# A transformer layer with 32 experts on one core: first gather from raw rows, logits by halves, a shorter root, and the overflow branch ahead of the scaling

## The chip, the core and the metric

The kernel runs on one core of a Trainium2 chip. It is timed on the device, in microseconds (us), as the median of several executions. Its engines are named as the profile names them: PE (TensorE matmul), PEld (TensorE's weight load, which overlaps PE), DVE (VectorE), ACT (ScalarE), POOL (GpSimd) and SP (SyncE, which here only issues DMAs; "SPq" is its queue, as "PEq" is PE's sequencer). A weight piece is 1 MB.

## The reference

One layer over 256 tokens of width 1024 (and 256 context tokens that only carry a state forward). All arrays are float32.

```python
sh1, sc1, gt1, sh2, sc2, gt2 = _split_mod(jax.nn.silu(c) @ w_mod + b_mod)
hx = _rms_norm(x, g_norm1) * (1.0 + sc1) + sh1
ux = hx @ w_in
...                     # a gated delta rule in two directions over ctx, then over x
mix_x = jnp.concatenate([_fourier(ux[..., :FOURIER_W]), _gated_out(ox, zx, g_out_norm)], axis=-1) @ w_out
x = x + gt1 * mix_x
h2x = _rms_norm(x, g_norm2) * (1.0 + sc2) + sh2
# mixture of experts: 32 experts, 4 for each token
logits = h @ w_router + b_router
top_v, top_i = lax.top_k(logits, 4)
gates = softmax(top_v)
# for each expert, on its tokens:
a = jnp.minimum(xb @ w_gate[e] + b_gate[e], 7.0)
u = jnp.clip(xb @ w_up[e] + b_up[e], -7.0, 7.0)
y = (a * sigmoid(1.702 * a) * (u + 1.0)) @ w_down[e] + b_down[e]
x = x + gt2 * sum(gate * y)
return _rms_norm(x, g_final)
```

Each of w_gate[e], w_up[e] and w_down[e] is 1024 x 1024, so the 32 experts have 384 MB of weights, and each is read once.

## The kernel before

The program has three parts.

**Prologue.** Modulation rows, norms, w_in, the delta rule, the Fourier products and w_out. It is cut into some forty small generators (`parts`), and a string `ORDER` and a table `EV` (which engine takes which copy out of PSUM) set the order in which they are recorded; a list scheduler of the framework then places their instructions by its own costs. The last parts are `X0` and `X1` (`routed`, L912): for each half `a` of 128 tokens it finishes x + gt1 * mix (L829, L830), multiplies by the norm's gain (L921: `xg`, the rows without the norm's factor), sums the squares on ScalarE (L922), turns `xg` by PE transposes (L927), copies the result (L199 or L201) and multiplies it by w_router (L933, 16 matmul records for 8 matmuls). `T` (`late_rows`, L939) spreads two rows of gt2 over the partitions with PE (L298), a ScalarE copy (L299) and GpSimd scalings (L946, L949).

**The hand-written bridge**, from L1217 on. From here the order on each engine is the written one. It takes the norm's factor `r` by `rsqrt` (L130: a first guess from the bits of the exponent and three Newton steps on VectorE, 11 operations in all). It then has PE multiply the rows by a diagonal matrix of `r` (`rows_`, L1228), while VectorE makes the logits (L1227), the top four and their mask (L1233 to L1239) and PE counts each token's rank within its expert (L1241 to L1245). `cast` (L1248) takes the scaled rows apart into three bfloat16 parts `h2s` whose sum is the row; the remainder for the next part is formed by PE (L1255, minus identity). `gather_first` (L1095) collects expert 0's tokens: a matmul with a one-hot matrix of the ranks, for 3 parts, 2 halves and 8 blocks of the width, 48 matmuls.

**The experts**, a loop of 32 (L1368), 64 token slots in the main path. Per expert: the gate's bias (L1123) and product (L1129, four weight pieces), its clip (L1135) and activation, the up product (L1129 again, four pieces), the gather for a later expert (L1091), the hidden rows turned (L1148), the down product (L1157, four pieces) and VectorE's scaling of its result by gt2/2 (L1422) into `yp`, which is later added into the token sums `yacc` by a matmul (L1207). An expert with more than 64 tokens takes a branch in two halves, for 32 further slots:

```python
if e >= EARLY:
    with tc.If(vs[e] > MAIN, preferred_fallthrough_block=False):
        hidden32(e, w)          # L1373, ahead of the gate's bias
...
if e >= EARLY:
    with tc.If(vs[e] > MAIN, preferred_fallthrough_block=False):
        down32(w)               # L1392, behind the up product
```

`hidden32` (L1162) builds a one-hot (L1073, L1075), gathers (L1091), does gate and up together (L1176, 64 matmuls), clips and activates (L1180 to L1184), then turns the gates (L1148) and the hidden rows and copies them. `down32` (L1193) has the down product (L1196).

**The weights** are loaded by SyncE alone, in order (`load_chunk`, L969), into 19 places that are used in turn. Most are old buffers of the prologue; one of them is the block "mm". SyncE waits until the last reader of a place is done, then issues the load and goes on to the next piece; all later pieces stand behind it.

Of the kernel before, what the change touches and what calls it, by code (L numbers as in the profile page):

```python
# [20 lines left out]
D = 1024  # L21
# [71 lines left out]
for _n, _w in (("c", 8), ("cc", 8), ("g1", 8), ("conv", 60), ("gout", 1), ("alog", 16), ("dtb", 16), ("br", 32)):  # L93
# [15 lines left out]
EV = {"fm0": "s", "mh01": "g", "ft1": "v", "md06": "v", "fm2": "s", "iu014": "v", "iu002": "s", "vn00": "s", "xT100": "v", "iu105": "s", "ip01": "v", "xh00": "s", "md04": "v", "xT110": "v", "md03": "v", "vn11": "v", "kT011": "v", "mh10": "v", "ir00": "s", "vv01": "s", "fa2": "s", "vv12": "v", "iu113": "s", "ix00": "s", "ft0": "s", "md05": "s", "fm3": "v", "xT010": "v", "md15": "v", "ir10": "v", "vv11": "v", "ir01": "s", "md02": "s", "iu104": "v", "iu004": "s", "md07": "v", "qg0": "s", "md17": "v", "xh10": "v", "mod0": "v", "kT101": "s", "iu103": "s", "xh11": "v", "mod2": "v", "ip00": "v", "xh01": "v", "xT011": "s", "cv100": "s", "xT001": "s", "mh00": "g", "cv201": "v", "iz11": "s", "cv113": "s", "cv103": "v", "iu112": "s", "iu111": "v", "cv010": "s", "fa1": "s", "kT111": "s", "qg1": "v", "ip10": "v", "vv10": "s", "iu011": "s", "qg2": "s", "iu114": "s", "fm1": "v", "cv211": "s", "cv213": "s", "cv013": "v", "md14": "s", "iu115": "v", "fa3": "v", "ip11": "v", "cv210": "v", "cv110": "v", "md00": "s", "cv212": "s", "ix10": "s", "xT000": "s", "md01": "s", "ix11": "v", "mh11": "g", "vv00": "v", "iu101": "v", "iu102": "v", "vn10": "s", "cv112": "v", "iz01": "v", "ix01": "v", "abT0": "v", "cv012": "v", "cv101": "s", "md11": "s", "mod1": "v", "qg3": "s", "iu005": "v", "xT101": "v", "md13": "s", "vv02": "s", "cv111": "v", "xT111": "s", "fa0": "v", "iu003": "s", "g21": "v", "md12": "s", "vv03": "v", "vn01": "s", "mh101": "s", "cv200": "s", "mh100": "v", "mh111": "g", "cv202": "s", "ir11": "g", "md10": "v", "g20": "s", "mh110": "v", "vv13": "s", "gT00": "v", "cv102": "v", "gT10": "v", "cv011": "v", "iz10": "s", "iu012": "s", "md16": "v", "mh011": "v", "iz00": "g", "cv203": "s", "mh001": "s", "mr24": "v", "mr25": "g", "mr23": "g", "mr27": "v", "mr10": "v", "kT110": "v", "mr26": "v", "gT11": "s", "mh010": "s", "kT010": "v", "kT100": "s", "mr11": "g", "mh000": "s", "mr22": "v", "iu015": "v", "mr14": "g", "iu001": "s", "mr21": "v", "gT01": "v", "iu013": "v"}  # L109
# [5 lines left out]
def body(ctx, tc, x, cx, sv, rows, cf, mk, w_mod, w_in, w_ab, w_out, w_router, w_exp, b_gate, b_up, b_down,  # L115
# [15 lines left out]
    def rsqrt(dst, v, scale, eps, mul=1.0):  # L131

        n = v.shape[-1]
        w = small.tile([128, n], F32, name="rsw")
        r = small.tile([128, n], F32, name="rsr")
        t = small.tile([128, n], F32, name="rst")
        nc.vector.tensor_scalar(w, v, scale, eps, op0=OP.mult, op1=OP.add)  # L137
        nc.vector.tensor_scalar(r.bitcast(I32), w.bitcast(I32), -0.5, float(0x5f3759df), op0=OP.mult, op1=OP.add)  # L138
        for i in range(3):
            nc.vector.tensor_tensor(t, r, r, OP.mult)  # L140
            nc.vector.scalar_tensor_tensor(t, t, -0.5, w, op0=OP.mult, op1=OP.mult)  # L141
            nc.vector.scalar_tensor_tensor(dst if i == 2 and mul == 1.0 else r, t, 1.5, r, op0=OP.add, op1=OP.mult)  # L142
        if mul != 1.0:
            nc.vector.tensor_scalar(dst, r, mul, None, op0=OP.mult)
# [752 lines left out]
    pl = None  # L897
# [14 lines left out]
    def routed(a):  # L912
        nonlocal pl
# [4 lines left out]
        for f in range(2):  # L918
# [20 lines left out]
    def late_rows():  # L939
# [3 lines left out]
        tmp = part("zfb", 0, D)  # L943
        for i in range(2):
            spread(tmp[:, 512 * i:512 * i + 512], mods[2], 64 + 32 * i)
            nc.gpsimd.tensor_scalar(g2h[64 * i:64 * i + 64], tmp[64 * i:64 * i + 64, 512 * i:512 * i + 512], 0.5, None,  # L946
                                    op0=OP.mult)
            for j in (2 * i, 2 * i + 1):
                nc.gpsimd.tensor_scalar(g2q[32 * j:32 * j + 32], tmp[32 * j:32 * j + 32, 256 * j:256 * j + 256], 0.5, None,  # L949
                                        op0=OP.mult)  # L950
# [93 lines left out]
    nib = keep.tile([128, 128], BF, name="nib")  # L1044
    nc.gpsimd.tensor_scalar(nib, ident, -1.0, None, op0=OP.mult)
# [49 lines left out]
    def gather_first(p, s, a):  # L1095

        for k in range(8):
            nc.tensor.matmul(p[:, k], h2s[:, s, a, 128 * k:128 * k + 128], ohs[0][:, a, 0], start=(a + s + k == 0),
                             stop=(a + s == 3), skip_group_check=True)
# [386 lines left out]
```

## Time and profile before

| | |
|---|---|
| median of 3 runs | 1300.39 us (1294.61 to 1303.88) |
| the profiled execution's own time | 1300.49 us |
| its span in the trace | 1298.4 us |
| PE busy | 1177.8 us, 91% |
| DVE, ACT, POOL busy | 415.8, 177.9, 91.8 us |
| mean granted clock of PE | 0.97 |
| moved by SyncE's DMA queue | 446.79 MB |

The span is the time from the first to the last record of the trace. The granted clock is the share of full speed that the chip allows TensorE. A busy share is an average over stages with different limits, so it doesn't say what ends the kernel; the rows below do. Times in the rows are counted from the span's start.

### The profile page before, as it was taken

To read this page: it belongs to the slowest core of one execution; us is meant where nothing else is said; L and a number is where in the kernel's file an instruction comes from. 1 tells how busy PE (TensorE), PEld (TensorE's weight loads), DVE (VectorE), ACT (ScalarE), POOL (GpSimd) and SP (SyncE) were. 2 spreads that over 40 slices of the span, in tenths; PEclk is the share of its full clock that TensorE was granted. 3 is DMA by queue.
4 is the path that set the end of the run, shared out by engine and by line. 5 is a ranking of instruction groups with operands and counts; after the bars stand their busy time and mean duration, and the time that the engine had idled before them with its cause. 6 is when DMAs were issued, how large, how long until landed. Compare 5 with 4: busy or idle time off the path is not lost. (4 is left out here: it accounts for less than half of the span.)

```text
span 1298.4 us, 17968 instructions
## 1 busy us (share of the span) xinstructions
PE 1177.8 (91%) x7381; PEld 534.3 (41%) x7381; DVE 415.8 (32%) x877; ACT 177.9 (14%) x338; POOL 91.8 (7%) x84
## 2 busy tenths in 40 slices
PE   6989988999989998989998998999789999998995
PEld 3767766665333333333332333333233333333322
DVE  2499879756311222111121211221122121221112
ACT  2165545111200000000000000000000000000001
POOL 1032544312000000000000000000000000000000
PEclk8999999999989999999999999999889999999998
DMA  9711353766799998899999999999999999999993
GB/s 383 273 33 67 120 174 111 288 249 238 313 355 418 420 419 328 354 420 418 418 421 418 420 419 419 419 420 419 419 420 421 419 420 419 419 420 419 418 416 116
DMA packets 65155, 450.60 MB, mean 347 GB/s; under 512 B 9220, under 2 KB 9608, under 8 KB 11000
## 3 DMA queue, kind: packets, MB, share of 16 engines
q1 hardware_dynamic: 64048, 446.79, 84.7%
q8 instruction: 106, 1.74, 0.5%
q10 hardware_dynamic: 904, 1.67, 0.3%
q14 instruction: 33, 0.27, 0.1%
q0 software_dynamic: 64, 0.13, 0.0%
HBM read 447.51 MB, written 1.05 MB: 345 GB/s over the span
## 5 line engine op out<-in xcount | busy, mean ns | idle before, releaser
L1129 PE MATMUL pg<-w,schT 128*64 128x512 f32 x1024 | 240.7, 616 | 17.7 <-issue 17.2
L1129 PE MATMUL pu<-w,schT 128*64 128x512 f32 x1024 | 229.4, 592 | 2.2 <-DMA w<-in_w_exp 2.1
L1157 PE MATMUL pd<-w,scA 128*64 128x512 f32 x1024 | 228.0, 598 | 1.1 <-ACTq L1373 0.7
L1129 PEld LDWEIGHTS pg<-w,schT 128*64 128x64 f32 x1024 | 74.9, 142 | 162.3 <-issue 153.9
L1129 PEld LDWEIGHTS pu<-w,schT 128*64 128x64 f32 x1024 | 73.1, 137 | 145.5 <-issue 131.5
L1157 PEld LDWEIGHTS pd<-w,scA 128*64 128x64 f32 x1024 | 70.9, 137 | 145.0 <-issue 136.7
L1422 DVE TENSOR_TENSOR xnat<-pd,qn 64x512 f32<-64x512 f32 x64 | 44.1, 688 | 269.6 <-PE pd L1157 269.1
L1135 DVE TENSOR_SCALAR schT<-pg 128x512 f32<-128x512 f32 x32 | 22.1, 692 | 247.1 <-PE pg L1129 247.1
L1136 ACT ACTIVATE scvnc<-schT 128x512 f32<-128x512 f32 x32 | 20.1, 630 | 547.6 <-DVE schT L1135 547.6
L1141 DVE TENSOR_SCALAR scvnc<-pu 128x512 f32<-128x512 f32 x32 | 22.1, 692 | 150.7 <-PE pu L1129 150.7
L1091 PEld LDWEIGHTS <-h2s 128*128 128x128 bf16 x864 | 45.2, 98 | 48.7 <-PEq L1392 40.3
L1207 PE MATMUL y<-xnat,scgm 128*128 128x512 f32 x136 | 61.3, 593 | 2.3 <-DVE xnat L1201 2.3
L1149 ACT ACTIVATE scA<-pg 128x512 f32<-128x512 f32 x32 | 19.1, 597 | 276.4 <-PE pg L1148 276.3
L507 PE MATMUL u<-hT,w 128*128 128x256 f32 x192 | 52.8, 402 | 0.0
L1091 PE MATMUL m<-scA,h2s 128*128 128x128 bf16 (+1 forms) x480 | 27.2, 212 | 12.5 <-PEq L1392 7.7
L507 PEld LDWEIGHTS u<-hT,w 128*128 128x128 f32 x192 | 33.2, 191 | 8.1 <-issue 4.3
L1207 PEld LDWEIGHTS y<-xnat,scgm 128*128 128x128 f32 x136 | 24.4, 190 | 27.7 <-issue 26.6
L317 ACT ACTIVATE w<-w,cst 128x256 f32<-128x256 f32 x80 | 33.9, 501 | 11.7 <-DMA w<-in_w_mod 11.7
L1082 DVE TENSOR_TENSOR schT<-m,sh2c 128x512 f32<-128x512 f32 (+2 forms) x33 | 22.2, 675 | 38.0 <-PE m L1091 37.3
L1123 PE MATMUL pg<-bgu,idb 96*64 96x512 bf16 x64 | 13.4, 417 | 21.3 <-PEq L1373 17.5
L1091 PE MATMUL m<-scgm,h2s 128*128 128x128 bf16 (+1 forms) x384 | 22.6, 215 | 8.9 <-PEq L1392 8.2
L318 POOL TENSOR_TENSOR w<-w 128x1024 f32<-128x1024 f32 x10 | 24.3, 2426 | 87.4 <-ACT w L317 87.4
(368 smaller groups left out, 1097.4 us busy)
## 6 DMA issues: line engine op xcount, KB each, us to landing
w<-in_w_exp SPq DMA_DIRECT2D x384, 1024.0 KB, 19.8
w<-in_w_mod SPq DMA_DIRECT2D x24, 1024.0 KB, 7.5
w<-in_w_in SPq DMA_DIRECT2D x6, 1024.0 KB, 6.4
w<-in_w_out SPq DMA_DIRECT2D x4, 1024.0 KB, 8.9
wk<-in_w_in SPq DMA_DIRECT2D x2, 1024.0 KB, 13.5
wv<-in_w_in SPq DMA_DIRECT2D x2, 1024.0 KB, 12.2
w<-in_cx SPq DMA_DIRECT2D x2, 512.0 KB, 5.1
xnat<-in_x SPq DMA_DIRECT2D x4, 256.0 KB, 12.8
```

Source lines behind the costliest of these rows:

```text
L317: nc.scalar.activation(w[:, k], w[:, k], AF.Copy, scale=sil[:, k, 0:1])
L318: nc.gpsimd.tensor_tensor(w[:, 0:4], w[:, 0:4], w[:, 4:8], OP.add)
L507: nc.tensor.matmul(p[:, c, :], w[c2][:, k, 128 * c:128 * c + 128], hT[:, k, 256 * n:256 * n + 256], start=(k == 0), stop=(k == 7))
L1082: nc.vector.tensor_tensor(dst[:, k0:k1], p, sh2c[:, k0:k1, None].to_broadcast([128, k1 - k0, p.shape[-1]]), OP.add)
L1091: nc.tensor.matmul(p[:, i], h2s[:, s, a, 128 * k:128 * k + 128], o[a], start=(s + a == 0), stop=(s + a == 3))
L1129: nc.tensor.matmul(p[64 * g:64 * g + 64], xg[:, k], w[k // 2][:, k % 2, 512 * g:512 * g + 512], start=False, stop=(k == 7), skip_group_che ...
L1135: nc.vector.tensor_scalar(a, p, 7.0, None, op0=OP.min)
L1136: nc.scalar.activation(hs_, a, AF.Tanh, scale=0.851)
L1141: nc.vector.tensor_scalar(hu_, p, 7.0, -7.0, op0=OP.min, op1=OP.max)
L1157: nc.tensor.matmul(p[64 * g:64 * g + 64], hT_[:, k, 64 * i:64 * i + 64], w[8 + 2 * i + k // 2][:, k % 2, 512 * g:512 * g + 512], start=(i ...
L1207: nc.tensor.matmul(yacc[a][g], ot[:, a, :], y[:, g, :], start=False, stop=False, skip_group_check=True)
L1422: nc.vector.tensor_tensor(yp[MAIN * j:MAIN * j + MAIN, g, :], p[hs], g2h[hs], OP.mult)
```

## The change

Six edits.

1. `routed` multiplies each turned half of the rows by its half of w_router at once, into the token sums' own PSUM (`yacc`), in place of all eight blocks at the end.
2. `late_rows` moves from the prologue's string into the bridge. PE spreads the two rows as before, and ScalarE scales them straight out of PSUM; GpSimd has no part in it.
3. `rsqrt` has nine operations in place of eleven (twelve, where a factor was applied).
4. The diagonal product, the copies behind it and the minus identity go. The first gather takes the raw rows `xg` in float32, with a one-hot `ohr` that holds the norm's factor where it held 1: 16 matmuls, four and four before the gate's product and eight within it. `ohr` lies in the block "mm".
5. The rows are taken apart into the three bfloat16 parts behind expert 0's gate product, by ScalarE and VectorE alone (`split`).
6. `hidden32(e + 1)` stands at the end of expert e, ahead of the scaling. Its gates and the turning of its hidden rows move into `down32`.

```diff
-    "H13 Fo E w Fo O0 O1 Fo w Lo Fo O0 X1 X0*2 w*2 X1 X0 T P w X1 X0 w X0 w*7 ")
+    "H13 Fo E w Fo O0 O1 Fo w Lo Fo O0 P X1 X0*2 w*2 X1 X0 w X1 X0 w*8 ")
...
-        for i in range(3):
-            nc.vector.tensor_tensor(t, r, r, OP.mult)
-            nc.vector.scalar_tensor_tensor(t, t, -0.5, w, op0=OP.mult, op1=OP.mult)
-            nc.vector.scalar_tensor_tensor(dst if i == 2 and mul == 1.0 else r, t, 1.5, r, op0=OP.add, op1=OP.mult)
-        if mul != 1.0:
-            nc.vector.tensor_scalar(dst, r, mul, None, op0=OP.mult)
+        c = 0.375 * mul
+        nc.vector.tensor_tensor(t, r, r, OP.mult)
+        nc.vector.scalar_tensor_tensor(t, t, -0.5 * c, w, op0=OP.mult, op1=OP.mult)
+        nc.vector.scalar_tensor_tensor(r, t, 1.5 * c, r, op0=OP.add, op1=OP.mult)
+        nc.vector.tensor_tensor(t, r, r, OP.mult)
+        nc.vector.scalar_tensor_tensor(t, t, 1.0 / (c * c), w, op0=OP.mult, op1=OP.mult)
+        nc.vector.scalar_tensor_tensor(t, t, -10.0 / 3.0, t, op0=OP.add, op1=OP.mult)
+        nc.vector.scalar_tensor_tensor(dst, t, 5.0, r, op0=OP.add, op1=OP.mult)
...
-            yield
-        if a == 0:
-            pl = bank("t", 2, 32)
-        for k in range(8):
-            nc.tensor.matmul(pl[:, a], xgT[:, k, :], wr[:, k, :], start=(k == 0), stop=(k == 7))
-        yield
+            for k in range(4 * f, 4 * f + 4):
+                nc.tensor.matmul(yacc[0][a][:, :32], xgT[:, k, :], wr[:, k, :], start=(k == 0), stop=(k == 7),
+                                 skip_group_check=True)
+            yield
...
+    def gather_first(p, ks):
+
+        for i, k in enumerate(ks):
+            for a in range(2):
+                nc.tensor.matmul(p[:, i], xgs[a][:, 128 * k:128 * k + 128], ohr[:, a], start=(a == 0), stop=(a == 1),
+                                 skip_group_check=True)
+
+    def split(a, f):
+
+        x, fs = xgs[a][:, 512 * f:512 * f + 512], slice(512 * f, 512 * f + 512)
+        nc.scalar.activation(x, x, AF.Copy, scale=r[:, a:a + 1])
+        yield
+        nc.vector.tensor_copy(h2s[:, 0, a, fs], x)
+        nc.vector.tensor_tensor(x, x, h2s[:, 0, a, fs], OP.subtract)
+        yield
+        nc.scalar.activation(h2s[:, 1, a, fs], x, AF.Copy)
+        yield
+        nc.vector.tensor_tensor(x, x, h2s[:, 1, a, fs], OP.subtract)
+        yield
+        nc.scalar.activation(h2s[:, 2, a, fs], x, AF.Copy)
+        yield
...
-        gates_turned(og, ovg)
-        p = mps.tile([128, 4, 64], F32, name="m")
+        return oh
+
+    def down32(e, w, oh):
+        gates_turned(gated(e, 1, oh, 4), ovg)
+        p = mps.tile([128, 4, 64], F32, name="pg")
...
+        next(parts["T"])
...
+        ohr = part("mm", 0, 2, MAIN)
+        for a in range(2):
+            nc.vector.tensor_scalar(ohr[:, a], io1[:, :MAIN], rk[:, a, 0:1], r[:, a:a + 1], op0=OP.is_equal, op1=OP.mult)
...
-            times(pg_, w[0:4], xg)
+                for p, ks in firsts:
+                    shifted(xg, p, ks)
+                times(pg_, w[0:4], xg, range(0, 2))
+                p = mps.tile([128, 4, MAIN], F32, name="pd")
+                gather_first(p, range(4, 8))
+                shifted(xg, p, range(4, 8))
+                times(pg_, w[0:4], xg, range(2, 8))
+                ohs[0] = onehot(oh_[0], 0, 2, 0, MAIN)
+                todo = [split(a, f) for a in range(2) for f in range(2)]
+                for i in range(len(todo) + 4):
+                    for j_, g in enumerate(todo):
+                        if 0 <= i - j_ < 5:
+                            next(g)
+            else:
+                times(pg_, w[0:4], xg)
...
             load_ahead(4)
+            if e + 1 < E:
+                with tc.If(vs[e + 1] > MAIN, preferred_fallthrough_block=False):
+                    ohov = hidden32(e + 1, weights_[e + 1])
             for g, hs in enumerate(halves):
                 nc.vector.tensor_tensor(yp[MAIN * j:MAIN * j + MAIN, g, :], p[hs], g2h[hs], OP.mult)
```

PE's instructions at the end of the prologue, in the order of the kernel before. `u` are the output product's tiles, `t` with `mm,cfk` the spread rows, `t` with `xg` the transposes, `t` with `gm` or `vec` the logits, `y` the diagonal product:

```order
L826 MATMUL u<-w,mixG 128x512
L298 MATMUL t<-mm,cfk 128x512 x2
L826 MATMUL u<-w,mixG 128x512 x4
L927 MATMUL t<-cfk,xg 128x128 x4
L933 MATMUL t<-mm,gm 128x32 x8
L927 MATMUL t<-cfk,xg 128x128 x4
L933 MATMUL t<-mm,vec 128x32 x8
```

The same place in the changed kernel, where the logits are L930 and the spread rows L944, both in the token sums' tiles `y`:

```order
L828 MATMUL u<-w,mixG 128x512
L930 MATMUL y_2937<-mm,gm 128x32 x4
L930 MATMUL y_2938<-mm,vec 128x32 x4
L828 MATMUL u<-w,mixG 128x512 x4
L927 MATMUL t<-cfk,xg 128x128 x4
L930 MATMUL y_2937<-mm,gm 128x32 x4
L927 MATMUL t<-cfk,xg 128x128 x4
L930 MATMUL y_2938<-mm,vec 128x32 x4
L944 MATMUL y_2939<-mm,cfk 128x512
L944 MATMUL y_2940<-mm,cfk 128x512
```

Half of each half's logits now stand ahead of the last output product, and the spread rows behind the last logits.

VectorE's instructions at the first branch, from the last step of expert 0's gathers on, before (`xnat<-pd,qn` is the scaling, `scgm` and `scA` the one-hot):

```order
L1082 TENSOR_TENSOR schT<-m,sh2c 128x512
L1422 TENSOR_TENSOR xnat<-pd,qn 64x512 x2
L1373 COMPARE_AND_BRANCH
L1373 UNCONDITIONAL_BRANCH
L1073 TENSOR_SCALAR scgm<-rk 128x1
L1075 TENSOR_TENSOR scA<-cfk,scgm 128x32
```

And in the changed kernel, through the whole branch:

```order
L1078 TENSOR_TENSOR schT<-m,sh2c 128x512
L1412 COMPARE_AND_BRANCH
L1412 UNCONDITIONAL_BRANCH
L1069 TENSOR_SCALAR scgm<-rk 128x1
L1071 TENSOR_TENSOR scA<-cfk,scgm 128x32
L1069 TENSOR_SCALAR scgm<-rk 128x1
L1071 TENSOR_TENSOR scA<-cfk,scgm 128x32
L1078 TENSOR_TENSOR scgm<-m,sh2c 128x256
L1191 TENSOR_SCALAR schT<-m 64x512
L1193 TENSOR_SCALAR scvnc<-m 64x512
L1194 SCALAR_TENSOR_TENSOR schT<-schT 64x512
L1195 SCALAR_TENSOR_TENSOR schT<-scvnc,schT 64x512
```

The scaling, which waits for the down product, stood ahead of the one-hot; now it stands behind the whole branch.

## Rows read from the trace of the kernel before

**Rows 1.** The page's slices of 32.5 us: DMA rate in each.
```profile
GB/s 383 273 33 67 120 174 111 288 249 238 313 355 418 420 419 328 354 420 418 418 421 418 420 419 419 419 420 419 419 420 421 419 420 419 419 420 419 418 416 116
```
**Rows 2.** Waits of SyncE's queue: who was waited for, total us, times, longest.
```profile
SPq L969 <- PE pd L1157: 115.7, 46, 12.5
```
**Rows 3.** Stretches of 25 us: PE, PEld, DVE, ACT, POOL busy; PEclk, DMA share, GB/s.
```profile
350.00:375.00 25.00, 20.12 (x138) 8.47 (x138) 3.81 (x9) 0.60 (x1) 0.95 (x1) 0.86 0.88 339
475.00:500.00 25.00, 19.89 (x160) 7.01 (x158) 5.51 (x13) 1.40 (x3) 0.00 (x0) 0.86 0.78 322
500.00:525.00 25.00, 23.52 (x170) 9.91 (x168) 5.54 (x11) 1.61 (x3) 0.00 (x0) 1.00 0.84 337
950.00:975.00 25.00, 19.92 (x154) 7.27 (x152) 5.51 (x13) 1.40 (x3) 0.00 (x0) 0.86 1.01 421
```
**Rows 4.** Timeline of the bridge: start us, us, instructions, idle before and its releaser.
```profile
311.92 1.88 PE L298 MATMUL t<-mm,cfk 128*128 128x512 f32 x4
...
313.63 3.60 PE L826 MATMUL u<-w,mixG 128*128 128x512 f32 x8
...
320.53 2.36 PE L933 MATMUL t<-mm,vec 128*128 128x32 f32 x16
...
320.73 0.60 ACT L199 ACTIVATE vec<-t 128x512 f32<-128x512 f32 x1 [0.77 <-PE t L927]
...
322.93 0.41 DVE L1227 SCALAR_TENSOR_TENSOR rt<-t,st,mm 128x32 f32<-128x32 f32 x2 [0.38 <-PE t L933]
...
324.52 0.20 DVE L1239 CAST mkb<-rt 128x64 bf16<-128x64 f32 x1
...
326.62 0.23 PE L1241 MATMUL u<-mkb,strb 128*128 128x32 bf16 x1
...
326.80 2.89 PE L1228 MATMUL y<-xg,mm 128*128 128x512 f32 x4
...
334.64 7.09 PE L1129 MATMUL pg<-w,schT 128*64 128x512 f32 x32 [0.44 <-DVE schT L1082]
```
**Rows 5.** Timeline of expert 0 behind its gate product, columns as before.
```profile
341.78 0.69 DVE L1135 TENSOR_SCALAR schT<-pg 128x512 f32<-128x512 f32 x1 [6.73 <-PE pg L1129]
...
346.54 0.14 DVE L1286 TENSOR_SCALAR cnt<-over 1x1 int32<-1x1 f32 x1
...
352.29 1.56 PE L1091 MATMUL m<-scgm,h2s 128*128 128x64 bf16 x48
...
354.18 0.63 PE L1148 MATMUL pg<-cfk,schT 128*128 128x128 f32 x4 [0.33 <-PE m L1091]
```
**Rows 6.** Timeline of expert 5's first half branch, to its gate product.
```profile
480.18 1.39 DVE L1422 TENSOR_TENSOR xnat<-pd,qn 64x512 f32<-64x512 f32 x2 [9.82 <-PE pd L1157]
...
482.04 1.70 PE L1091 MATMUL m<-scA,h2s 128*128 128x32 bf16 x48 [1.91 <-DVE scgm L1073]
...
484.63 9.27 PE L1176 MATMUL m<-w,scgm 128*32 128x512 f32 x64
...
497.50 7.04 PE L1129 MATMUL pg<-w,schT 128*64 128x512 f32 x32
```
**Rows 7.** Short stretches, columns as in the stretches of 25 us.
```profile
396.00:400.00 4.00, 4.00 (x20) 1.33 (x22) 0.69 (x1) 0.00 (x0) 0.00 (x0) 1.00 1.02 420
482.00:484.00 2.00, 1.60 (x48) 1.52 (x49) 0.86 (x5) 0.00 (x0) 0.00 (x0) 0.57 1.01 422
490.00:492.00 2.00, 2.00 (x24) 0.50 (x16) 0.00 (x0) 0.00 (x0) 0.00 (x0) 1.00 1.02 422
```
**Rows 8.** Timeline of PE at the branches of experts 1 and 2.
```profile
367.89 0.64 PE L1123 MATMUL pg<-bgu,idb 96*64 96x512 bf16 x2 [3.80 <-issue]
...
368.31 9.39 PE L1129 MATMUL pg<-w,schT 128*64 128x512 f32 x32
...
395.90 0.41 PE L1123 MATMUL pg<-bgu,idb 96*64 96x512 bf16 x2 [0.63 <-PEq L1373]
```
**Rows 9.** Lines by form: one of the root's operations in the prologue; mean in ns.
```profile
L140 DVE TENSOR_TENSOR rst<-rsr 128x8 f32<-128x8 f32 x9 | 4.4, 491 | 0.1
```

More of the change, by code (lines that the diff above doesn't have):

```diff
@@ L896, in body @@
     xgs = {}
-    pl = None
     sh2c = keep.tile([128, 8], F32, name="sh2c")
@@ L912, in routed @@
     def routed(a):
-        nonlocal pl
         xg = tail.tile([128, D], F32, name="xg", tag="A", bufs=2)
@@ L942, in late_rows @@
         g2h, g2q, gatT = late[:, :512], late[:, 512:768], late[:, 768:]
-        tmp = part("zfb", 0, D)
         for i in range(2):
[L945 to L950, printed above, removed]
+            p = yacc[1][i]
+            r = 64 + 32 * i
+            nc.tensor.matmul(p, ident[:, r:r + 1].to_broadcast([128, 128]), mods[2], start=True, stop=True)
+            nc.scalar.activation(g2h[64 * i:64 * i + 64], p[64 * i:64 * i + 64], AF.Copy, scale=0.5)
+            for j in (0, 1):
+                q = slice(64 * i + 32 * j, 64 * i + 32 * j + 32)
+                nc.scalar.activation(g2q[q], p[q, 256 * j:256 * j + 256], AF.Copy, scale=0.5)
         nc.gpsimd.memset(gatT, 0.0)
@@ L1043, in body @@
     nc.gpsimd.tensor_copy(strb, C("strict"))
-    nib = keep.tile([128, 128], BF, name="nib")
-    nc.gpsimd.tensor_scalar(nib, ident, -1.0, None, op0=OP.mult)
     io1 = C("iota1")
@@ L1093, in gather @@
         shifted(dst, p, ks)
[L1095 to L1099, printed above, removed]
+    def gather_first(p, ks):
[16 more added lines that the diff above has]
+        yield
     def gated(e0, ne, oh, dup):
@@ L1166, in hidden32 @@
         xo = xov_.rearrange("p (k s) -> p k s", k=8)
-        og = gated(e, 1, oh, 4)
         gather(xo, oh, range(8))
@@ L1217, in body @@
         next(parts["X1"])
-        next(parts["X1"])
         r = st[:, 12:14]
@@ L1221, in body @@
         rsqrt(r, r, 1.0 / D, EPS)
-        dg = part("mm", 0, 2, 128)
-        fs = [slice(512 * g, 512 * g + 512) for g in range(2)]
+        next(parts["T"])
         for a in range(2):
-            nc.scalar.activation(dg[:, a], ident, AF.Copy, scale=r[:, a:a + 1])
-        for a in range(2):
-            nc.vector.scalar_tensor_tensor(lg[:, a], pl[:, a], r[:, a:a + 1], brr, op0=OP.mult, op1=OP.add)
-        rows_ = lambda a: [nc.tensor.matmul(yacc[a][g], dg[:, a], xgs[a][:, fs[g]], start=True, stop=True)
-                           for g in range(2)]
-        rows_(0)
+            nc.vector.scalar_tensor_tensor(lg[:, a], yacc[0][a][:, :32], r[:, a:a + 1], brr, op0=OP.mult, op1=OP.add)
         top = st[:, 14:16]
@@ L1352, in body @@
     with tc.manual_schedule(engines={ET.PE, ET.Activation, ET.DVE, ET.SP, ET.Pool}):
-        first = mps.tile([128, 8, MAIN], F32, name="m")
-        cast(0, 1, 0, "s")
-        cast(1, 0, 1, "s")
-        cast(0, 1, 1, "v")
-        gather_first(first, 0, 0)
-        cast(1, 1, 0, "v")
-        gather_first(first, 1, 0)
-        cast(2, 0, 0, "s")
-        cast(1, 1, 1, "v")
-        cast(2, 0, 1, "s")
-        gather_first(first, 0, 1)
-        cast(2, 1, 0, "s")
-        gather_first(first, 2, 0)
-        cast(2, 1, 1, "v")
-        gather_first(first, 1, 1)
+        firsts = []
+        for nm, ks in (("m", range(0, 2)), ("pu", range(2, 4))):
+            firsts.append((mps.tile([128, len(ks), MAIN], F32, name=nm), ks))
+            gather_first(*firsts[-1])
         for e in range(E):
@@ L1371, in body @@
             xg = xgs_[pair][:, :, MAIN * j:MAIN * j + MAIN]
-            if e >= EARLY:
-                with tc.If(vs[e] > MAIN, preferred_fallthrough_block=False):
-                    hidden32(e, w)
             pg_ = mps.tile([128, 512], F32, name="pg")
@@ L1377, in body @@
             if e == 0:
-                gather_first(first, 2, 1)
-                for ks in (range(0, 2), range(2, 8)):
-                    shifted(xg, first[:, ks[0]:ks[-1] + 1], ks)
-            times(pg_, w[0:4], xg)
+                for p, ks in firsts:
[13 more added lines that the diff above has]
+                times(pg_, w[0:4], xg)
             a = gate_part(pg_)
@@ L1392, in body @@
                 with tc.If(vs[e] > MAIN, preferred_fallthrough_block=False):
-                    down32(w)
+                    down32(e, w, ohov)
             up_part(pu_, a)
```

29 lines of the change are left out of this document (8 added, 21 removed).

## The prediction

> **What bounds the kernel now.** I read the page's slices first, then the DMA queue's own waits, then the timeline at the three places where weights stop flowing.
>
> The slices show two halves [rows 1]. In the first ten, 32.5 us each, little is loaded and PE works off the prologue. From the thirteenth on the weights come at some 420 GB/s, 2.5 us for each of the 384 pieces of 1 MB, except in slices 16 and 17 (328 and 354). So the end is "when the weights begin to flow, plus all weights at full speed, plus the pauses, plus a fixed tail". What a change saves on PE counts only where PE keeps the loads waiting.
>
> Where is that? The weights lie in a ring of 19 pieces, and SyncE waits for PE to finish with a piece before it loads the next into its place. SyncE waited 115.7 us for down products to release one [rows 2]. The 25 us stretches place the pauses [rows 3]: at 350 the DMA share is 0.88, from 475 on 0.78 and 0.84, against 1.01 in full flow. That is 0.13 x 25 = 3.2 us in the first, and (0.23 + 0.17) x 25 = 10 us in the second. The second pause is expert 5, the first with more than 64 tokens. At the other such expert PE is disturbed as much, yet the stretch at 950 shows a share of 1.01: by then PE is ahead of the loads. So only three things pay: an earlier expert 0, a shorter expert 5, a shorter tail.
>
> **The change part by part.**
>
> *Logits and late rows.* The last output product waited for two broadcasts, which held PE from 311.92 to 313.63, 1.7 us [rows 4]. The change moves them behind the logits and puts eight logit matmuls there. Sixteen records, eight matmuls, took 2.36 us, 0.295 each. So xg is ready 2.36 - 1.71 = 0.65 us later.
>
> *From xg to expert 0.* PE's transposes of the last half ended at 320.7 and end at 321.4; ScalarE's copy takes 0.60 [rows 4], so 322.0; four logit matmuls, 1.18, so 323.2. The root, which VectorE had done before its logit step at 322.93, is two steps shorter, and these matmuls cover it. From the logits to the mask took 322.93 to 324.72 on VectorE and takes 1.8 again: 325.0. Meanwhile PE does the two broadcasts (1.88, to 325.1), which cover that wait. Before, the ranks stood on PE behind the diagonal product of the rows and began at 326.62, 1.9 us after their mask. Now they follow at once: 325.1 + 0.35 = 325.45 (before, the product behind them began 0.18 after the first of them, which takes 0.23). Ranks and two scaled one-hots on VectorE are three steps like the mask's cast, 0.20 and a gap each: 0.75, to 326.2. The first gather, in float32, is 16 matmuls of the logits' kind, 0.295 each: four and four before the first product (2.36), about 0.4 for the bias, so expert 0's gate starts at 329.0, against 334.64. The other eight gather matmuls (2.36) stand between its k = 1 and k = 2, so the gate ends at 329.0 + 7.1 + 2.4 = 338.5 against 341.73: **3.2 us earlier**.
>
> *A page on the weight load.* The sixteen logit records of 2.36 us are float32 stationaries that are hardly covered [rows 4], and the gather that goes was bfloat16, 48 matmuls in 1.56 [rows 5]. The Trainium skill (TensorE: Matmul & The Clock Gate, "Weight-path perf modes" and "LDWEIGHTS") says that float32 has no fast weight load and that a load takes its columns over 1.2 GHz. It speaks against this change, and the trace agrees in kind. By its figure a load of 128 columns takes 107 ns and the two of a matmul 0.213 us, an estimate that would make the gather 1.3 us shorter and the sum 1288.5. I keep the row's 0.295.
>
> *Splitting the rows behind expert 0.* Three ScalarE and three VectorE passes over 512 columns for each of four halves. VectorE's passes are bounded by the 0.69 of its 512-column operations [rows 5], twelve make 8.3 us; ScalarE's by 0.60 [rows 4], 7.2 beside them. They start when the gather has read the rows, at about 333.4, and end at about 342. They stand ahead of the gate's clip and the softmax in both queues. From that clip to the last count took 341.78 to 346.68, the up part after it 1.4, 6.3 us together; PE needs the result at 354.18 - 3.2 = 351.0 [rows 5]. So they may end as late as 344.6: covered, 2.6 us to spare, and nothing is added.
>
> *SyncE and GpSimd.* The piece that goes into the "mm" block waited for the diagonal product, which ended at 329.7 [rows 4]; now it waits for the gather's last read, about 333.3, with the next releases behind it on SyncE. The later releases, all 3 to 5 us earlier, make up for that before the pause at 370; without them it would cost 3.6 us. The scaling of the late rows leaves GpSimd, and the piece that waited for it no longer does, but the "mm" piece stands next: nothing.
>
> *The branch ahead of the scaling.* Where it isn't taken, PE's order is the same: nothing. At expert 5, VectorE first scaled (from 480.18, 1.39 us) and only then built the one-hot; PE idled 1.91 us, and the granted clock fell to 1.2 GHz (0.57 from 482 to 484, 1.00 again from 490) [rows 6, 7]. So 64 matmul records took 9.27 us, where 24 go in 2 us at 2.4 GHz: 5.3, a price of 4.0. Now the one-hot is built while PE still multiplies. Rows that bound the idle: 0.63 us at the branch of expert 2 [rows 8] and 1.91 here; I take 0.63, since nothing PE waits for is left. After those 0.63 the clock was 1.00 (396 to 400) [rows 7]. Then the gather 1.56, shift and bias 0.9 (from the gather's end at 483.74 to 484.63), products 5.3, the gate's bias 0.4: 8.8 us. What followed the products, 493.9 to 497.50 with PE nearly idle, leaves this place. Before, it took 480.18 to 497.50, 17.3: **8.5 us less**; 4.5 if the clock falls all the same. The turned gates and hidden rows come back ahead of the second half of the branch: two short groups of transposes, bounded by the 0.63 of four full ones [rows 5], say 0.4 each, and ScalarE's copy of 0.6: **1.4 us more**. The scaling comes later on VectorE; what it feeds on PE stands behind the next expert's products.
>
> *Shorter roots.* The last root is on the tail: two small VectorE steps of 0.2, **0.4 us less**. Seven stand in the prologue. Some took much longer there, 0.49 us a step in the mean [rows 9]; three roots of that kind and four of 0.2 make 14 steps, 4.5 us at most. Against it the planner moves the up bias's splitting, three ScalarE and two VectorE passes over 1024 columns, 3 x 1.2 + 2 x 1.38 = 6.4 us by the 0.60 and 0.69 for half as many, to where PE runs the Fourier products. I take 0, between 4.5 us less and 6.4 more, since PE was the busy one there and its work is unchanged.
>
> **Sum.** -3.2 - 8.5 + 1.4 - 0.4 = -10.7. The loads can give that back: the 3.2 come from the start, and 7.1 of the 10 us of pauses at expert 5. From the profiled execution's 1300.49, which lies 0.1 from the median of the three runs (1300.39): **1289.8 us**.
>
> **The rivals.**
> - *The clock falls at expert 5 all the same* (short matmuls before and after the one-hot). For it: the idle stays in two pieces. Against: at expert 2 the clock stayed. 4.0 us of the gain go: 1293.8. Chance 0.13.
> - *The first jump no longer stalls.* PE idled 3.80 us at its first branch, and the gate after it took 9.39 instead of 7.04 us; at the next branch it idled 0.63 [rows 8]. So a jump's price depends on where in the program it lands, and PE's program has 104 instructions less ahead of it. Against it: nothing in the change shortens that jump. If the stall goes, PE wins 3.2 + 2.3, of which the 3.2 us pause at 350 limits the loads' part to some 4: 1285.8. The Trainium skill (Runtime: NRT & Kernel Launch, "Instruction fetch mechanics") says that a taken branch out of the fetched blocks waits for a DMA; the two rows agree. Chance 0.12.
> - *One more such stall* before expert 5: 3.8 + 2.3 us: 1295.9. Chance 0.12.
> - *The splits come late.* If each pass waits for the other engine's, 24 passes of 0.65 last 15.6 us, to 349.0, 4.4 over the limit, and PE's idle costs half clock, 4.0: 1298.2. Chance 0.06.
> - *Slower: the moved bias passes* at 255 to 280 us. If they hold up copies that PE waits for, twice by the 1.9 us of expert 5, PE loses 6.4 us and twice 4.0 of half clock: 1304.2. It decides from 10.7 us on. Against it: only the copies that stand behind them on the same engine can be late. Chance 0.05.
>
> **How the numbers follow.** The forecast has 0.52, with a range of its own from 1286 to 1293. To hold 8 in 10 the range takes in the stalls on either side: 1283 to 1298. One per cent, about what a measurement of this kernel can tell from no change (its runs spread from 1294.61 to 1303.88), is 13 us: faster by more needs 1287.4. The vanished stall and the lower part of the forecast with a gain in the prologue give 0.27; slower by more is the last rival, 0.04; the rest 0.69.
>
> **What would show it.** Expert 0's gate at 329 and ending near 338.5; expert 5's gate some 9 us after the fourth's down product, with the clock at 2.4 GHz; no DMA pause at 480 to 500, a short one near 515; the first branch still near 3.8 us. It is wrong if the prologue's products before 300 us move by more than 2 us, if the turned-hidden transposes of expert 0 wait for VectorE, or if DMA pauses elsewhere.

## The result and the profile after

The changed kernel takes **1288.94 us** (median of 4, 1284.3 to 1290.18) against 1300.36 before; the ratio is 0.991, 95% interval 0.9881 to 0.9939. A second set of runs gave 1290.09 (0.9914, 0.9885 to 0.9944). Forecast was 1289.8. The profiled execution took 1288.59, with a span of 1286.7 against 1298.4.

The slices and the long stretches of the changed kernel, in the columns of [rows 1, 3]:

```profile
GB/s 383 279 34 67 112 184 112 291 250 277 205 420 418 419 419 403 390 410 420 419 419 418 419 419 419 419 420 419 419 421 420 419 419 419 420 419 420 419 417 125
```

```profile
350.00:375.00 25.00, 23.34 (x165) 9.72 (x165) 5.00 (x10) 1.23 (x2) 0.95 (x1) 1.00 1.01 419
475.00:500.00 25.00, 24.03 (x174) 8.34 (x177) 6.26 (x11) 2.03 (x4) 0.00 (x0) 1.00 1.01 421
500.00:525.00 25.00, 20.13 (x133) 8.44 (x125) 5.54 (x11) 0.98 (x2) 0.00 (x0) 1.00 0.97 391
525.00:550.00 25.00, 23.71 (x125) 10.14 (x123) 5.24 (x9) 1.23 (x2) 0.00 (x0) 1.00 0.98 376
950.00:975.00 25.00, 24.47 (x170) 8.12 (x166) 5.87 (x10) 2.02 (x4) 0.00 (x0) 0.96 1.01 421
```

The two pauses are gone from 350 and 475 (DMA shares 1.01); small ones came at 500 and 525, and the eleventh slice is worse than before (205, was 313). Weight by weight, the pieces counted from 0: piece 22 landed 2.7 us *later* than before (352.86, was 350.17), piece 40 3.9 earlier, piece 90 12.9 earlier, piece 110 9.7 earlier, the last one 10.65 earlier (1268.48, was 1279.13). The tail, from that landing to the end of the span, gave 1.0 more (18.23 us, was 19.23).

**The bridge** (timeline of PE, columns as in [rows 4]):

```profile
318.96 0.63 PE L927 MATMUL t<-cfk,xg 128*128 128x128 f32 x4 [0.33 <-DVE xg L921]
320.28 1.78 PE L930 MATMUL y<-mm,vec 128*128 128x32 f32 x8 [0.69 <-ACT vec L201]
321.87 3.76 PE L944 MATMUL y<-mm,cfk 128*128 128x512 f32 x4
325.42 0.23 PE L1246 MATMUL y<-mkb,strb 128*128 128x32 bf16 x1
...
326.52 1.94 PE L1095 MATMUL m<-mm,xg 128*128 128x64 f32 x8 [0.76 <-DVE mm L1254]
328.26 1.91 PE L1095 MATMUL pu<-mm,xg 128*128 128x64 f32 x8
...
330.53 3.62 PE L1141 MATMUL pg<-w,schT 128*64 128x512 f32 x8
334.08 2.00 PE L1095 MATMUL pd<-mm,xg 128*128 128x64 f32 x16
336.01 5.37 PE L1141 MATMUL pg<-w,schT 128*64 128x512 f32 x24
```

```profile
314.00:320.00 6.00, 4.31 (x22) 2.51 (x20) 3.46 (x10) 1.09 (x3) 0.00 (x0) 1.00 0.76 274
320.00:334.00 14.00, 12.96 (x43) 7.55 (x43) 3.91 (x23) 3.40 (x8) 0.00 (x0) 0.52 0.08 33
```

PE was busy 4.31 of the 6 us up to 320, and from then to 334 the granted clock was 0.52, near 1.2 GHz. The spread rows took 3.76 us for the 1.88 of [rows 4]; eight gather records took 1.94, while sixteen took 2.00 once the clock was back. From the start of the last transposes (318.96) to the end of expert 0's gate (341.38) it took 22.42 us, against 21.66 before. DMA stood nearly still from 320 to 334 (share 0.08).

**The splits** of the rows end in time, though their last ScalarE pass ends at 344.45, where the forecast had about 342. The clip starts at 343.70 and the count at 348.47, and PE takes the next gather at 351.93 without a wait (answers to [rows 5]).

```profile
343.70 0.68 DVE L1147 TENSOR_SCALAR schT<-pg 128x512 f32<-128x512 f32 x1
...
348.47 0.14 DVE L1279 TENSOR_SCALAR cnt<-over 1x1 int32<-1x1 f32 x1
...
351.93 1.56 PE L1087 MATMUL m<-scgm,h2s 128*128 128x64 bf16 x48
353.83 0.63 PE L1160 MATMUL pg<-cfk,schT 128*128 128x128 f32 x4 [0.34 <-PE m L1087]
```

**The first branch** no longer stalls PE (answers to [rows 8]): 0.57 us in place of 3.80, and the gate behind it 7.03 in place of 9.39.

```profile
364.32 0.41 PE L1135 MATMUL pg<-bgu,idb 96*64 96x512 bf16 x2 [0.57 <-PEq L1412]
364.56 7.03 PE L1141 MATMUL pg<-w,schT 128*64 128x512 f32 x32
```

**Expert 5** (answers to [rows 6]): the gather begins before the fourth down product has ended (473.62), and the gate 9.25 us after that end, where it was 17.37.

```profile
473.56 1.36 PE L1087 MATMUL m<-scA,h2s 128*128 128x32 bf16 x48
...
475.65 7.05 PE L1187 MATMUL m<-w,scgm 128*32 128x512 f32 x64
...
482.87 7.03 PE L1141 MATMUL pg<-w,schT 128*64 128x512 f32 x32
...
517.17 2.74 PE L1141 MATMUL pg<-w,schT 128*64 128x512 f32 x11
...
522.75 4.88 PE L1141 MATMUL pg<-w,schT 128*64 128x512 f32 x21 [2.84 <-issue]
```

The last two rows are new: within expert 6's gate PE stops for 2.84 us and waits for nothing that the profile shows; a packet of the instruction queue started at 520.2, 0.3 us into the stop. The smaller rate at 525 is its echo: it is gone in two kernels without the stop (420 and 423 GB/s, "Three matmuls that keep PE busy" and "As many instructions, without the cover" below). The one at 500 is not: both of them have it too (391 and 392). It lies at 510 to 514, ahead of the stop, where SyncE has waited 13.8 us for a down product to release a place.

### The profile page after: what moved, and what is told of

Its sections match the earlier page's. It is cut to its first block, busy times and chain, and to the rows that moved or that the text cites. A ratio compares the mean times of both kernels' runs of the same rounds, so it can differ in the third digit from the quotient of the medians.

```text
span 1286.7 us, 17920 instructions
## 1 busy us (share of the span) xinstructions
PE 1170.0 (91%) x7349; PEld 540.1 (42%) x7349; DVE 422.2 (33%) x868; ACT 182.2 (14%) x345; POOL 83.9 (7%) x77
## 5 line engine op out<-in xcount | busy, mean ns | idle before, releaser
L1141 PE MATMUL pg<-w,schT 128*64 128x512 f32 x1024 | 235.0, 605 | 12.7 <-issue 12.0
L1141 PEld LDWEIGHTS pu<-w,schT 128*64 128x64 f32 x1024 | 75.8, 137 | 148.1 <-issue 123.0
L1078 DVE TENSOR_TENSOR schT<-m,sh2c 128x512 f32<-128x512 f32 (+1 forms) x32 | 21.7, 680 | 39.1 <-PE m L1087 37.2
L1135 PEld LDWEIGHTS <-idb 96*64 96x64 bf16 x128 | 7.9, 108 | 58.6 <-issue 58.2
```

The costliest lines, as they stand in the source:

```text
L1078: nc.vector.tensor_tensor(dst[:, k0:k1], p, sh2c[:, k0:k1, None].to_broadcast([128, k1 - k0, p.shape[-1]]), OP.add)
L1135: nc.tensor.matmul(p[64 * g:64 * g + 64], idb[:, e:e + 1].to_broadcast([96, 64]), b[:, 512 * g:512 * g + 512], start=True, stop=False, ski ...
L1141: nc.tensor.matmul(p[64 * g:64 * g + 64], xg[:, k], w[k // 2][:, k % 2, 512 * g:512 * g + 512], start=False, stop=(k == 7), skip_group_che ...
```

## The experiments

Medians are of each kernel's own runs; "before" was 1300.9, 1300.1 and 1301.4 us beside the three groups of runs. Two distances are compared over all profiles, since the start of the weights shifts from execution to execution. **Bridge**: from the start of the last transposes to the end of expert 0's gate. **Pace**: from that end to the landing of weight piece 200.

### One part at a time

**The old root in the changed kernel.** Edit: in `rsqrt`,

```diff
-        c = 0.375 * mul
...
-        nc.vector.scalar_tensor_tensor(dst, t, 5.0, r, op0=OP.add, op1=OP.mult)
+        for i in range(3):
+            nc.vector.tensor_tensor(t, r, r, OP.mult)
+            nc.vector.scalar_tensor_tensor(t, t, -0.5, w, op0=OP.mult, op1=OP.mult)
+            nc.vector.scalar_tensor_tensor(dst if i == 2 and mul == 1.0 else r, t, 1.5, r, op0=OP.add, op1=OP.mult)
...
```

> The changed kernel with the old root (three Newton steps) at all places. In the changed kernel the first weight piece was issued at 248.67 us, before at 251.02. Theory: the shorter root brought these 2.3 us and 0.4 of the tail; then the first piece goes back to about 251 and the time to 1291.5. Rival: the 2.3 us come from elsewhere (PE's clock in the first 25 us, the planner's other order); then the first piece stays near 248.7 and the time is 1289.3.

Measured: 1285.10 us (ratio 0.9868, 0.9847 to 0.9889); first piece issued at 249.17. It is not slower, and by the medians some 4 us faster, but the interval overlaps the changed kernel's (from 0.9881). Neither theory holds. Over all profiles the prologue, from the first product of the value weights to the last transposes, took 263.5, 263.9, 264.1, 265.2, 266.9 and 267.1 us with the old root, and 265.6 to 267.8 in eight with the shorter one, in whose prologue the planner puts the instructions in another order (265.1 and 266.5 in the mean). The shorter root gives its 0.40 us on the tail (2.14 to 1.74 from its first operation to its last one's end) and no gain in the prologue.

**The scaling back ahead of the branch.**

```diff
+            for g, hs in enumerate(halves):
+                nc.vector.tensor_tensor(yp[MAIN * j:MAIN * j + MAIN, g, :], p[hs], g2h[hs], OP.mult)
             if e + 1 < E:
                 with tc.If(vs[e + 1] > MAIN, preferred_fallthrough_block=False):
                     ohov = hidden32(e + 1, weights_[e + 1])
-            for g, hs in enumerate(halves):
-                nc.vector.tensor_tensor(yp[MAIN * j:MAIN * j + MAIN, g, :], p[hs], g2h[hs], OP.mult)
```

> The changed kernel with the scaling put back ahead of the branch's first half; gates and turned rows stay in the second half. Theory: VectorE's scaling ahead of the one-hot cost expert 5 the 1.9 us idle and the half clock; from the fourth down product's end to the fifth gate it takes about 15 us in place of 9.25, and the time is about 1293.5. Rival: taking the gates and the turning out of that place was all; then it takes 10 us and the time is 1289.5. At the first branch PE idles 0.6 us as in the changed kernel if the place in the program decides, 3.8 us as before if VectorE's order does.

Measured: 1292.39 us (0.9933, 0.991 to 0.9957), and 12.49 us from the fourth down product's end to the fifth gate. So it lies between the two theories: of the 8.1 us by which expert 5 became shorter, 3.2 are the order. The other 4.9 are the gates and the turning, which left the place, and a clock that recovered sooner. The timeline of PE shows the order's part:

```profile
470.27 1.67 PE L1087 MATMUL m<-scA,h2s 128*128 128x32 bf16 x48 [1.90 <-DVE scgm L1069]
...
472.84 7.84 PE L1187 MATMUL m<-w,scgm 128*32 128x512 f32 x64
```

The idle of 1.90 us is back, but the half clock cost only 7.84 - 7.05 = 0.8 us, where it cost 9.27 - 7.05 = 2.2 in [rows 6]. At the first branch PE idled 0.58 us: VectorE's order was not the cause of that stall.

**The branch's edit alone in the kernel before.** Besides these lines, `hidden32` and `down32` are those of the change.

```diff
-            if e >= EARLY:
-                with tc.If(vs[e] > MAIN, preferred_fallthrough_block=False):
-                    hidden32(e, w)
...
+            if e + 1 < E:
+                with tc.If(vs[e + 1] > MAIN, preferred_fallthrough_block=False):
+                    ohov = hidden32(e + 1, weights_[e + 1])
```

> The kernel before with the branch's edit alone. Theory: expert 5 gains 8.1 us ahead of its gate and loses 1.4 behind it, the loads keep most of it: 1294.5. Rival: the loads give it back behind expert 5, since they flow at full rate anyway: 1298.5. The first branch idles 3.8 us if its stall hangs on where the jump lands, and PE's program is as before up to there.

Measured: 1294.59 us (0.9956, 0.9932 to 0.9981), as the theory had it; expert 5 takes 9.25 again. But the first branch stalled 0.46 us, not 3.80, with another 0.95 us within the gate behind it:

```profile
363.71 0.41 PE L1123 MATMUL pg<-bgu,idb 96*64 96x512 bf16 x2 [0.46 <-PEq L1419]
...
365.93 6.23 PE L1129 MATMUL pg<-w,schT 128*64 128x512 f32 x28 [0.95 <-issue]
```

From expert 0's down product to the end of this gate it took 10.36 us, 15.06 before. A stall of 2.59 us stood in expert 4's gate instead, and from expert 1's gate to the fourth down product it took 5.4 us longer than before. The two nearly cancel, so it is partly luck that the time agrees with the theory.

**The branch's edit and the root, without the new bridge.** The kernel before with the last diff and, in `rsqrt`, with

```diff
-        for i in range(3):
...
+        c = 0.375 * mul
...
```

> The kernel before with the branch's edit and the shorter root, so the changed kernel without the new bridge (first gather, splits, logits by halves, late rows). Theory: the bridge ran at half clock and is worth nothing by itself; this kernel differs from the changed one by the first branch's stall alone: 1293 if PE idles 3.8 us there, 1288 if 0.6. Rival: the bridge is worth the 3.2 us of the forecast: 1296 with the stall, 1292 without.

Measured: 1295.97 us (0.9959, 0.9944 to 0.9974), with 0.45 us at the first branch and 0.81 in the gate behind it: above what either theory gives without the stall. The new bridge is all that separates it from the changed kernel (with one copy, `gT10` in `EV`, that went from VectorE to ScalarE and that the list of edits doesn't name). By the medians it is worth 7.0 us, more than its forecast. But a stall stands in expert 4's gate here too: from expert 1's gate to the fourth down product it took 107.66 us, against 102.03 in the changed kernel. So the 7.0 us are not the bridge's own. Bridge: 20.09 us here and 20.58 in the kernel before it, against 22.42 in the changed kernel's profile. Either that profile is not typical, or the gain is not in the bridge.

### The clock in the bridge

**The changed kernel again.** No edit.

> The changed kernel unchanged, for a second profile on another chip and as the control of the three beside it. In the first profile PE ran at half clock from 321 to 334 us and expert 0's gate ended at 341.4; the kernel with the scaling first, the same up to expert 0's end, had half clock only from 321 to 324 and its gate ended at 336.1. Theory: where this spell ends differs from execution to execution of one program; then the gate ends between 335 and 342, other than 341.4 by over 1 us, and the time is 1288.9 within 2. Rival: the spell belongs to the program; then it ends at 334 and the gate at 341.4 again, within 1 us, counted from the same prologue.

Measured: 1290.09 us. The bridge took 18.02 us in this profile, not 22.42. Rows of PE, and the clock (columns as in [rows 4, 7]):

```profile
323.55 0.63 PE L927 MATMUL t<-cfk,xg 128*128 128x128 f32 x4 [0.33 <-DVE xg L921]
...
325.85 3.59 PE L944 MATMUL y<-mm,cfk 128*128 128x512 f32 x4
...
332.45 1.89 PE L1141 MATMUL pg<-w,schT 128*64 128x512 f32 x8
```

```profile
326.00:330.00 4.00, 3.55 (x10) 1.32 (x9) 1.86 (x13) 1.75 (x5) 0.00 (x0) 0.61 0.07 29
330.00:334.00 4.00, 3.69 (x26) 2.45 (x26) 1.06 (x5) 1.43 (x4) 0.00 (x0) 1.00 0.00 0
```

The spell of half clock begins behind the same idle times, but ends by 330 here. So where it ends differs between executions of one program. The expectation judged it by the time of the gate's end alone. That was 341.57, like 341.38, and would have said the opposite, because the whole prologue was 4.6 us later in this execution. Counted from the last transposes, as the rival's own words ask, the theory holds.

**Three matmuls that keep PE busy.**

```diff
+            if f == 1:            # in routed, ahead of the last logits of each half
+                nc.tensor.matmul(yacc[1][a], ident[:, 64:65].to_broadcast([128, 128]), mods[2], start=True, stop=True)
...
+        nc.tensor.matmul(yacc[0][1], ident, xgs[0][:, :512], start=True, stop=True, skip_group_check=True)  # behind the ranks
```

> The changed kernel with three matmuls whose results nobody reads: one of 0.94 us at full clock in each of PE's two idle times between the last transposes and their logits (0.94 and 0.69 us), and one behind the ranks (0.76 us idle). Theory: PE's idle times there bring the half clock; then the granted clock stays 1.00 from 310 to 340, expert 0's gate ends 17 us after the last transposes' start (22.4 in the changed kernel) and the time falls by the 2 to 5 us that the spell cost: 1285.5. Rival: the spell comes whatever PE does there; then the three add 0.4 to 1 us at full, 1.5 at half clock: 1290.

Measured: **1284.18 us** (0.9873, 0.9845 to 0.9901). The clock stayed at full speed, and the bridge took 16.40 us:

```profile
320.98 0.63 PE L927 MATMUL t<-cfk,xg 128*128 128x128 f32 x4 [0.34 <-DVE xg L921]
...
323.20 1.96 PE L946 MATMUL y<-mm,cfk 128*128 128x512 f32 x4
...
328.26 1.88 PE L1143 MATMUL pg<-w,schT 128*64 128x512 f32 x8
```

```profile
320.00:334.00 14.00, 13.66 (x83) 8.36 (x84) 7.46 (x36) 5.22 (x11) 0.00 (x0) 1.00 0.30 104
```

PE does more work than in the changed kernel and is done sooner. Over all profiles the bridge took 17.82 to 22.65 us in the six with the new bridge and without these matmuls (the cover, from here on), each with a spell of half clock, and 16.40, 16.40 and 16.54 in the three with it, at full clock. With the old bridge it took 20.09 to 24.02 in five. But the stall in expert 6's gate was gone too, so the 5.9 us between the medians (1290.09 and 1284.18) are not all the clock's.

**As many instructions, without the cover.**

```diff
+        for i in range(3):        # behind the ranks alone
+            nc.tensor.matmul(yacc[0][1][:, 32 * i:32 * i + 32], ident, xgs[0][:, :32], start=True, stop=True, skip_group_check=True)
```

> The changed kernel with three matmuls of 32 columns behind the ranks, whose results nobody reads, where PE idles 0.76 us: as many instructions as the three that kept PE busy, but the two idle times ahead of them stay. With those three PE's 2.8 us stall within expert 6's gate was gone too. Theory: that stall hangs on the place in the program and goes here as well, while the half clock from about 321 us on stays: 1287.5, some 3 us above the kernel with the three long matmuls (1284.2). Rival: the whole 5.9 us came from the clock: 1290.

Measured: 1287.75 us (0.989, 0.9872 to 0.9909), as expected: the spell stayed (bridge 22.65) and the stall in expert 6 was gone (PE's rows; stretches as in [rows 3]):

```profile
323.18 3.76 PE L944 MATMUL y<-mm,cfk 128*128 128x512 f32 x4
...
518.69 7.04 PE L1141 MATMUL pg<-w,schT 128*64 128x512 f32 x32
```

```profile
500.00:525.00 25.00, 23.09 (x166) 9.78 (x168) 5.54 (x11) 0.98 (x2) 0.00 (x0) 1.00 0.97 392
525.00:550.00 25.00, 23.77 (x124) 8.98 (x122) 5.24 (x9) 1.23 (x2) 0.00 (x0) 1.00 1.02 423
```

Pace: 464.5, 465.6, 465.7 and 466.5 us in the four profiles with that stall (the changed kernel twice, the one-hot apart, the old root), 462.1 to 462.8 in the four without. So the stall is worth about 3 us to the loads. The cover is worth the rest: 2.2 us by the two ratios (0.989 and 0.9873), 3.6 by the medians. The intervals of these ratios overlap, so the gain in time is likely but not shown clear of noise; the clock and the shorter bridge are shown.

### The block "mm"

**The one-hot in another block.**

```diff
-        ohr = part("mm", 0, 2, MAIN)
+        ohr = xov_[:, :2 * MAIN].rearrange("p (a s) -> p a s", a=2)
```

> The changed kernel with the scaled one-hot in another block than mm. Weight piece 18, which goes into mm, was issued at 336.11 in the changed kernel and all loading stood still from 322 to 336. Theory: the piece now waits for the spread rows only, is issued some 10 us earlier, and is loaded while nothing else is: one piece, 2.5 us, is gained for all that follow: 1286.4. Rival: PE, not the loads, sets the pace until expert 8, and the gain is gone by then: 1288.9.

Measured: 1289.48 us (0.9915, 0.9887 to 0.9942), no clear gain on the 1290.09 of the unchanged program beside it (the control). Piece 18 was issued at 326.80, and piece 22 landed 8.5 us after the gate's end in place of 11.4 in the control. By piece 40 1.4 of these 3 us were left, by piece 90 none (184.3, 184.2 in the control). The rival holds: PE sets the pace up to there.

**Cover and one-hot apart.**

> The three matmuls and the one-hot apart together. Theory: both gains, the releases of expert 0's pieces earlier and one piece more in the idle time: 1283. Rival: the one covers the other, since either makes the loads earlier than PE wants them until expert 8: 1285.5. If neither works, 1289 to 1290.

Measured: 1280.53 us (0.9851, 0.9818 to 0.9885). Its interval overlaps that of the cover alone, and its pace is nearly the same (462.8, 462.4); that the one-hot adds anything is not shown.

**The same with the old root.** Edit: the three above.

> The three matmuls and the one-hot apart, with the old root. From the first product behind the modulation to the last transposes the prologue took 263.9 us with the old root and 265.6 to 267.7 with the shorter one, in which the planner orders the prologue otherwise. Theory: the old root's order is better by some 2 us, less 0.4 for the tail: 1279. Rival: the difference is the scatter of the prologue's clock, and the shorter root is worth its 0.4: 1281.

Measured: **1279.89 us** (0.9838, 0.9811 to 0.9866), the fastest; its interval lies below the changed kernel's. Between the two roots nothing is decided.

### The first branch

**The kernel before again.**

> The kernel before unchanged, for a second profile. Its first branch stalled PE for 3.80 us, and the gate product behind it took 9.39 us; in all changed kernels so far PE idled 0.6 us there. Theory: the stall belongs to the program: 3.8 us again, within 0.3, and a gate of more than 9 us. Rival: it comes and goes from execution to execution: 0.6 us.

Measured: 1299.44 us, one run; the stall is there again, with the half clock behind it (PE's rows; columns as in [rows 8]):

```profile
367.89 0.41 PE L1123 MATMUL pg<-bgu,idb 96*64 96x512 bf16 x2 [3.84 <-issue]
368.13 8.73 PE L1129 MATMUL pg<-w,schT 128*64 128x512 f32 x32
```

The gate was 8.73, not over 9: the stall belongs to the program, the length of the half clock to the execution.

**Three small matmuls in the kernel before.**

```diff
+        for i in range(3):        # ahead of rows_(1)
+            nc.tensor.matmul(yacc[1][1][:, 32 * i:32 * i + 32], ident, xgs[0][:, :32], start=True, stop=True, skip_group_check=True)
```

> The kernel before with three matmuls of 32 columns behind the ranks, whose results nobody reads: PE's program is three matmuls longer ahead of the first branch, the jump itself is as long as before. Theory: the stall hangs on the length of the jump, which the change shortened by moving the gates and the turning out of the branch's first half: 3.8 us again. Rival: it hangs on where the jump stands in the program: 0.6 us here, and the stall turns up at another place.

Measured: 1304.51 us, one run. The jump is as long as before, and most of its stall is gone:

```profile
368.84 0.41 PE L1123 MATMUL pg<-bgu,idb 96*64 96x512 bf16 x2 [1.18 <-issue]
369.08 7.04 PE L1129 MATMUL pg<-w,schT 128*64 128x512 f32 x32
...
699.58 0.64 PE L1123 MATMUL pg<-bgu,idb 96*64 96x512 bf16 x2 [6.61 <-issue]
```

1.18 us in place of 3.84, and the clock stays. A stall of 6.61 us stands at a branch 330 us later. The kernel before has one there too, of 4.24 and 4.52 us in its two profiles, but inside the gate behind that branch:

```profile
697.45 7.97 PE L1129 MATMUL pg<-w,schT 128*64 128x512 f32 x24 [4.52 <-issue]
```

So three matmuls move and change stalls far from where they stand. From expert 0's down product to the end of expert 1's gate it took 9.90 us here, with the long jump, and 10.36 with the branch's edit alone, with the short one. The place in the program decides, in single runs of each kernel at least.

## Why the prediction was right

The time came out as forecast, and so did what limits it: expert 5 and the loads. But the terms for expert 0 and for the first branch were wrong in the profile at hand, and a stall at expert 6 was not in the sum. Together these three came to 1.6 us (4.0 + 3.4 less 5.8), so it is in part luck that the number came within 1 us.

- **Expert 5: right, in compensating parts.** Forecast 8.8 us to the gate, measured 9.25 in all ten profiles of kernels with the whole edit. The idle of 0.63 did not come, since the gather waits for nothing. The 64 products take 7.05 us, not the 5.3 that I took from "24 records in 2 us" in [rows 7]. A stretch counts every record that runs in it, and records overlap: of the 24 only 16 began in those 2 us. So the price of the half clock was 2.2, not 4.0, and the rival on it was priced too high. The clock did not fall. The second half of the branch took 1.36 us more, forecast 1.4. The short pause forecast near 515 is the one at 510 to 514.
- **Expert 0: the order held, its clock didn't.** The forecast has 17.8 us from the last transposes to the gate's end. Two executions came close, 18.02 when the changed kernel ran again and 17.82 with the scaling first (the same program up to there), against 21.66 and 21.42 before. In the profile that came with the result it was 22.42, because the forecast carried the full-clock durations of the spread rows and the gate through a stretch ahead of which PE idles 1.7 us in 6. Even at 18.02 two errors offset each other: the spread rows took 3.59 us instead of 1.88, so the ranks began 1.3 us late, and the gather was cheaper. At full clock one of its matmuls measured 2.00 / 8 = 0.25 us, at half 0.48; I had 0.295. The estimate of 0.213 weighed beside it was too low.
- **The first branch: the step "nothing in the change shortens that jump" failed.** The rival that the stall goes was given 0.12 and happened: 15.06 and 14.26 us from expert 0's down product to the end of expert 1's gate before, 9.29 after. The sentence misreads the change, since edit 6 takes the gates and the turning out of the part that this jump skips. But three matmuls ahead of a jump of the old length gave 9.90, so it was the jump's place, as the rival said. At the same time one more such stall came, at expert 6 (2.84 us) and not before expert 5, where the opposite rival had it. Together they are some 2.4 us to the good (5.8 less 3.4).
- **Prologue 0, splits covered: right.** The first piece's 2.3 us at 250 us are scatter: the kernel unchanged issued it at 253.25 in its second profile. The planner's other order cost the prologue 1.4 us in the mean, within the scatter of both. The sentence on the "mm" piece was right as well: it was issued at 336.11, and that was made up for by piece 40.
- **What the loads give back: right.** In the profile, PE was 13.3 us ahead of before at expert 6's gate, 9.9 behind the new stall, and the last piece landed 10.65 earlier.

By terms, on PE, from the profiles of both kernels: prologue -1.1, bridge +0.8, first branch -5.8, experts 1 to 4 -0.4, expert 5 -8.1 and +1.4, expert 6's stall +3.4: -9.8 at expert 7's gate, where the measured difference is 548.64 - 558.49 = -9.85. The loads made it -10.65 and the tail -11.65. Of the tail's 1.0 us the root gave 0.40; the rest is not accounted for, as the tail takes 18.23 to 19.54 us in the eight profiles with the shorter root.

The Trainium skill (Runtime: NRT & Kernel Launch, "Instruction fetch mechanics") calls the crossing of a block's boundary in straight code mostly hidden. The stall in expert 6's gate stands within a product, not at a jump, and took 2.84 us while the weights flowed at 398 GB/s (517 to 528). The packet of the instruction queue that begins in it points to such a crossing, but that the stall is one is not shown. The Trainium skill (TensorE: Matmul & The Clock Gate, "What's actually happening") also says that the number of slow matmuls at a kernel's start varies from run to run; the spells of half clock in the bridge, of some 3 to 13 us with the same instructions, agree in kind.

## What to carry to other kernels

Before you price a stretch by rows, look at the granted clock that its neighbours had and at PE's idle time ahead of it: three matmuls that nobody reads kept the clock at 1.00 here, and the bridge took 16.40 to 16.54 us with them, 17.82 to 22.65 without. Before you credit an edit with a stall that went, move the program by three instructions and see whether it goes then too. And compare by distances within one trace, from the last common event, since the start of an execution alone shifts by more than most edits are worth.

## What was not expected of the hardware

Half clock at the start of an execution scatters too. It may be a good part of the scatter of the measured times (1284.3 to 1296.17 for the changed kernel alone), but two profiles don't show how much. The stretch of 30 to 40 us of one program, in two executions (the scaling first, whose prologue is the changed kernel's, and the changed kernel again):

```profile
30.00:40.00 10.00, 9.21 (x60) 7.31 (x56) 1.41 (x5) 1.75 (x3) 0.00 (x0) 0.96 1.05 301
```

```profile
30.00:40.00 10.00, 9.19 (x50) 5.66 (x49) 1.40 (x5) 1.59 (x3) 0.00 (x0) 0.50 1.05 300
```

With the clock at 0.96 the first product of the value weights began at 50.5 us, at 0.50 at 57.8. So the start, which edits of the bridge cannot reach, differs by 7.3 us between two executions, more than the bridge gained; whether cover of the same kind would help there was not tried.
